# A two-layer backbone on one core: layer 1's modulation from sums on the vector engine instead of matmuls on the tensor engine

## The chip, the cores and the metric

One core of one Trainium2 chip runs the whole program. The metric is the time of one execution on the device in microseconds (us). Kernel names and line numbers (L...) are those of the kernel before, unless said otherwise; after the change the lines from 291 on are some 34 higher.

## The reference, cut to what matters

Each of the two layers modulates its inputs by six vectors that depend on a conditioning vector alone. There are two streams of tokens, 128 context tokens and 256 latent tokens, each with one conditioning vector (`c_ctx` and `c`):

```python
def adaln(cond, w, bias):
    return (jax.nn.silu(cond) @ w + bias)[:, None, :]

for l in range(DEPTH):                                    # DEPTH = 2
    mod_ctx = adaln(c_ctx[None, :], w_ada[l], b_ada[l])   # w_ada[l]: 1024 x 6144
    mod_lat = adaln(c, w_ada[l], b_ada[l])
    xp, ... = residual_block(xp, mod_ctx, p, ...)
    xs, _ = residual_block(xs, mod_lat, p, ...)

def residual_block(x, mod, p, mixer):
    sh1, sc1, g1, sh2, sc2, g2 = jnp.split(mod, 6, axis=-1)
    y, extra = mixer(rmsnorm(x, p['norm1_g']) * (1 + sc1) + sh1)
    x = x + g1 * y
    h = rmsnorm(x, p['norm2_g']) * (1 + sc2) + sh2
    x = x + g2 * (jnp.square(jax.nn.relu(h @ p['w_ff1'])) @ p['w_ff2'])
    return x, extra
```

Everything is fp32. The feed-forward is 1024 to 4096 to 1024 features for 384 tokens in all. The modulation is a product of two rows (the two streams) with a 1024 x 6144 matrix, 24 MB for each layer.

## The kernel before

Tokens lie along the free dimension: `x[k]` is tile k of 8, 128 features by T = 384 tokens. A weight matrix comes in tiles of 128x1024 (512 KB): a DMA from SyncE into `raw` (3 buffers), a rounded copy `whi` on ScalarE (L147, 3 buffers) and the remainder `wlo` on VectorE (L148, 2 buffers). `mm3` (L150 to L153) then issues three matmuls for each 128x128 block of it: `whi` by the high part of the activations, `whi` by the low part, `wlo` by the high part. A weight tile is 8 blocks, so 24 matmuls.

**The feed-forward of a layer (L1074 to L1108).** FF1 has 32 output tiles of one weight tile each. After each, VectorE reads the PSUM bank (`fb` L1089, `fa` L1090), ScalarE does the relu and the square, and the result is split into `fh` and `fl`. FF2 has 8 output tiles d, each the sum of 32 blocks, so four weight tiles (c = 0 to 3); at the end of each, `residual` (L301) adds it to `x[d]` in two VectorE instructions. FF1 and FF2 take their PSUM banks from a pool of three, tag "g".

**Layer 1's modulation** is made beside layer 0's feed-forward by the generator `ada(l + 1, [0, 1, 2])` (L272 to L290): `next(more)` runs one step of it after each FF1 tile and after each c of FF2. There are 3 rounds of 2048 columns, each 8 k by 2 halves, so 48 steps. A step is one DMA of 512 KB into `araw` (2 buffers) and 4 fp32 matmuls on TensorE, each with a 128x32 weight (`cs`, the conditioning vectors: 2 of 32 columns are not zero) by 256 columns, into a quarter of the PSUM partitions of a "g" bank. A round holds that bank for its 16 steps. The last step of a round turns the bank on VectorE (`diag`, L285) and adds the bias (`mod`, L289). The modulation of layer 0 is made elsewhere, at the start (`mraw` tiles, in `lead`) and beside layer 0's merge.

**What sets the order.** Each engine runs its instructions in the order in which a scheduler has put them. SyncE's DMA issues are in order too: a transfer whose buffer isn't free yet holds those behind it. At the start of layer 1, `modulated` (L220 to L232) makes the normalised input as a chain of VectorE instructions (L227, L230) and ScalarE ones (L229) through the 8 feature tiles, and the first matmuls of the input projection follow it tile by tile.

Of the kernel before, what the change touches and what calls it, by code (L numbers as in the profile page):

```python
# [13 lines left out]
AF = mybir.ActivationFunctionType  # L14
ALU = mybir.AluOpType
# [3 lines left out]
P = 128  # L19
DM = 1024  # L20
KT = DM // P
T = 384
SEQ = 128
DEPTH = 2
# [15 lines left out]
Q_N1, Q_N2, Q_ADA, Q_GQ, Q_GKV, Q_CW, Q_ON, Q_SINK, Q_AL, Q_DT, Q_FG = 0, 8, 16, 64, 67, 69, 105, 106, 114, 122, 130  # L40
# [4 lines left out]
def trunk(ctx: ExitStack, tc: tile.TileContext, A, O):  # L45
    nc = tc.nc
    V, S, G, PE = nc.vector, nc.scalar, nc.gpsimd, nc.tensor
    count = [0]

    def mk(pool, shape, tag, dt=F32, bufs=None):  # L50
        count[0] += 1
        return pool.tile(list(shape), dt, name=f"{tag}_{count[0]}", tag=tag, bufs=bufs)
# [28 lines left out]
    sp = sbuf("small", 2)  # L81
    dp = ctx.enter_context(tc.tile_pool(name="scratch", bufs=2, space=DRAM))
    pg = psum("pg", 3)
# [4 lines left out]
    def bank(pool=None, tag="c"):  # L88
        return mk(pc if pool is None else pool, [P, 512], tag)
# [24 lines left out]
    prm = []  # L114
# [35 lines left out]
    def mm3(ps, wh, wl, rh, rl, start, stop):  # L150
        PE.matmul(ps, lhsT=wh, rhs=rh, start=start, stop=False)  # L151
        PE.matmul(ps, lhsT=wh, rhs=rl, start=False, stop=False)  # L152
        PE.matmul(ps, lhsT=wl, rhs=rh, start=False, stop=stop)  # L153

    def mm(ps, lhsT, rhs, start=True, stop=True):
        return PE.matmul(ps, lhsT=lhsT, rhs=rhs, start=start, stop=stop)  # L156
# [103 lines left out]
    cs = mk(cp, [P, KT, 32], "cs")  # L260
# [6 lines left out]
    mods = {}  # L267
    ada_pool = [None, "araw", 2]

    def ada(l, rounds):  # L270

        for r in rounds:  # L272
            ps = bank(pg, "g")
            for k in range(KT):
                for half in range(2):
                    c0 = r * 2048 + half * 1024
                    raw = mk(ada_pool[0], [P, 1024], ada_pool[1], bufs=ada_pool[2])
                    nc.sync.dma_start(raw, A["w_ada"][l, k * P:(k + 1) * P, c0:c0 + 1024])
                    rv = raw.rearrange("p (b g i) -> p g b i", b=8, g=4)
                    for g in range(4):  # L280
                        mm(ps[32 * g:32 * g + 32, half * 256:half * 256 + 256].rearrange("p (b i) -> p b i", b=8),
                           cs[:, k, :], rv[:, g], start=k + half == 0, stop=k + half == KT)
                    if k + half == KT:
                        tr = mk(sp, [P, 512], "diag", bufs=1).rearrange("p (b i) -> p b i", b=16)
                        V.transpose(out=tr.rearrange("p b i -> p (b i)"), in_=ps)  # L285
                        m = mods[l, r] = mk(sp, [P, 16, 2], f"mod{r}")
                        bias = prm[l][:, Q_ADA + 16 * r:Q_ADA + 16 * r + 16].unsqueeze(2).to_broadcast([P, 16, 2])
                        V.tensor_tensor(out=m, in0=tr[:, :, 0:2], in1=bias, op=ALU.add)
                    yield  # L289

    def gain(m, b0, l, off, tag):
# [132 lines left out]
    for l in range(DEPTH):  # L424
# [5 lines left out]
        else:  # L430
# [6 lines left out]
            for w in weights([A["w_small"][l], A["w_in"][l, 11]]):  # L437
                wh, wl = (t.rearrange("p (k c) -> p k c", k=KT) for t in w)
                M = wh.shape[2]
                ps = mk(pg, [P, 512], "g")[:M, :T + 2]  # L440
# [4 lines left out]
            for i, ps in enumerate(pss):  # L445
                M = ps.shape[0]
                t = mk(sp, [48, T], "kab", bufs=1) if i == 0 else mk(sp, [P, T], "sqacc", bufs=1)
                b = mk(sp, [P, 2], "eb")[:M]
# [57 lines left out]
        if l == 0:  # L506
            ps, kab = kab, mk(sp, [48, T], "kab", bufs=1)
# [54 lines left out]
        for k in range(7, 0, -1):  # L562
# [4 lines left out]
        g = mk(sp, [P, 3, 8], "gdec")  # L567
        V.scalar_tensor_tensor(out=g, in0=z, scalar=-1.0, in1=nea.unsqueeze(1).to_broadcast([P, 3, 8]),
                               op0=ALU.mult, op1=ALU.mult)
# [4 lines left out]
        for d in range(2):  # L574
            for i in range(3):
# [13 lines left out]
                        op0=ALU.mult)  # L589
# [113 lines left out]
        for which, dst in enumerate((keys, queries)):  # L703
# [11 lines left out]
            r = rsqrt(v, 12, 1.0)  # L715
            r2 = mk(sp, [P, 12], f"r2{which}", bufs=1)
            if which == 0:
# [4 lines left out]
                                in1=r2.rearrange("p (n h) -> p n h", n=3).unsqueeze(2).to_broadcast([P, 3, 2, 4]), op=ALU.mult)  # L722
# [29 lines left out]
        diag = blk()  # L752
        G.memset(diag[:, :, 24:32], 0.0)
        Mg, QK, qd, ekd, ge = {}, {}, {}, {}, {}
        for n in range(3):
            Es = []
            for d in range(2):
                gr = bank()
                for h in range(4):
                    j = 8 * n + 4 * d + h  # L760
                    for i in range(3):
                        mm(gr[:, h * P:(h + 1) * P], g16[i][:, j:j + 1].to_broadcast([P, P]), tri16[:, d, :],
                           start=h + i == 0, stop=h + i == 5)
# [20 lines left out]
            for d in range(2):  # L784
                M = Mg[n, d] = g4()
                for h in range(4):
                    V.scalar_tensor_tensor(out=M[:, h, :], in0=kk[:, h * P:(h + 1) * P],
                                           scalar=beta[:, n, 4 * d + h:4 * d + h + 1], in1=Es[d][:, h, :],
                                           op0=ALU.mult, op1=ALU.mult)
# [20 lines left out]
        for j in range(31):  # L810
            r, w = 31 - j, j + 1
            tmp = flat(h4())[:, :r * w].rearrange("p (a b) -> p a b", a=r)
            V.tensor_tensor(out=tmp, in0=Cb[:, j + 1:, j:j + 1].to_broadcast([P, r, w]),  # L813
                            in1=X[:, j:j + 1, :w].to_broadcast([P, r, w]), op=ALU.mult)
# [10 lines left out]
        for n in range(3):  # L825
            for d in range(2):
# [8 lines left out]
                for dst, c in ((X0T, (Xc, XcT)[d]), (X0, (XcT, Xc)[d])):  # L835
                    V.tensor_tensor(out=dst.rearrange("p h (b c) -> p h b c", b=4),  # L836
                                    in0=c[:, u0:u0 + 4, :].unsqueeze(2).to_broadcast([P, 4, 4, 32]),
                                    in1=bdmask.rearrange("p (b c) -> p b c", b=4).unsqueeze(1).to_broadcast([P, 4, 4, 32]),
                                    op=ALU.mult)
                ps = bank()  # L840
# [237 lines left out]
        rs2 = mk(fp, [P, T], "rs2")  # L1078
        S.copy(rs2, rstd_rows(squares(x), 1.0 / DM))
        NF = 32  # L1080
        ada_pool[:] = fp, "araw", 2
        more = ada(l + 1, [0, 1, 2]) if l + 1 < DEPTH else iter(())
        ws = weights(A["w_ff1"][l, t] for t in range(NF))
        ah, al = [], []
        for t in range(NF):
# [14 lines left out]
        for d in range(KT):  # L1100
            ps = mk(pg, [P, 512], "g")
            for c in range(4):
                wh, wl = (w.rearrange("p (k c) -> p k c", k=KT) for w in next(ws))
                for k in range(KT):
                    i = c * KT + k
                    mm3(ps[:, :T], wh[:, k, :], wl[:, k, :], ah[i], al[i], i == 0, i == NF - 1)
                next(more, None)
            residual(d, ps, mod2, KT)  # L1108
        ff.close()
# [136 lines left out]
```

## Time and profile before

| | |
|---|---|
| three runs | 1579.08, 1581.01, 1582.5 us; median 1581.01 us |
| the profiled execution | 1581.47 us |
| its span in the profile | 1579.7 us, so 1.8 us lie outside of it |
| mean granted clock of TensorE in it | 0.997 |
| layer 0's feed-forward in it | 521.1 to 830.0 us |
| steps of `ada` in that stretch | 48 |

The span goes from the first instruction to the last. An engine's busy time is the sum of its instructions; matmuls overlap, so that each shows some 0.34 us while one starts every 0.175 us. A line of the timeline reads: start, duration, engine, line, operation, output<-inputs, count, and in brackets the engine's idle time before it with what ended it. Adjacent equal instructions are joined as x2, x8 and so on; one fp32 matmul shows as two records. "PE" is TensorE, "PEld" its weight load, "DVE" VectorE, "ACT" ScalarE. A row of the windows gives the stretch, its length, the busy us (and instructions) of PE, PEld, DVE, ACT and POOL, the granted clock as a share of the full one, the busy share of the DMA engines, and GB/s. A row of the groups gives line, engine, operation, names, shapes and count, then the busy us, the mean ns of one, and the idle time before them.

### The profile page before, as it was taken

The page shows a single profiled execution, that of the slowest core. Times are in us where ns is not written, and L with a number is a line of the kernel's source. Part 1 is how long each engine was busy: PE and PEld are TensorE (multiplying, and loading weights), DVE is VectorE, ACT ScalarE, POOL GpSimd, SP SyncE. Part 2 cuts the span into 40 slices and gives each one's busy share as a digit, 9 for nine tenths or more (in the row PEclk, how much of TensorE's full clock was granted, in tenths as well). Part 3 has the DMA queues.
Part 4 walks back from the last instruction along what each step waited for, and adds up shares of the span by engine and source line. Part 5 has one row for each costly group of instructions (what it writes and reads, how often), then busy time and mean ns, then how long its engine had stood idle before and what let it go on. Part 6 is the DMA issues. An engine that isn't in the chain of part 4 may idle for free.

```text
span 1579.7 us, 25197 instructions
## 1 busy us (share of the span) xinstructions
PE 1542.1 (98%) x9844; PEld 1393.1 (88%) x9844; DVE 904.4 (57%) x2016; ACT 756.1 (48%) x1498; POOL 12.9 (1%) x34
## 2 busy tenths in 40 slices
PE   5999999999999999999999999999999999999998
PEld 3898798987879888888998987989978999999997
DVE  5677995565435644443338678964755565554332
ACT  3467633446424655532325566433565456664222
POOL 0000100000000000000000001000000000000000
PEclk9999999999999999999999999999999999999999
DMA  9532131243587566666444331312423334343332
GB/s 324 157 94 94 54 94 41 68 147 98 191 274 254 166 209 209 209 216 224 155 135 123 94 99 39 118 41 65 125 69 121 120 121 134 121 125 128 128 126 80
DMA packets 73942, 212.80 MB, mean 135 GB/s; under 512 B 8032, under 2 KB 23776, under 8 KB 73696
## 3 DMA queue, kind: packets, MB, share of 16 engines
q1 hardware_dynamic: 73824, 211.21, 41.9%
q8 instruction: 77, 1.26, 0.3%
q14 instruction: 41, 0.34, 0.1%
HBM read 204.59 MB, written 4.75 MB: 133 GB/s over the span
## 4 chain that ended last, share of the span: by engine, by line
PE 88%; DVE 6%; DMA 3%; ACT 1%; issue 1%; SPq 0%; DVEq 0%; ACTq 0%
PE g L151 23%; PE g L153 22%; PE g L152 22%; PE c L156 9%; PE g L156 3%; PE f L156 3%; PE o L156 2%; PE f L409 2%; DMA araw<-in_w_ada_dram 2%; DVE wlo L148 1%; DVE h L813 1%; DVE blk L815 1%; DMA mraw<-in_w_ada_dram 1%; PE c L151 1%; PE c L153 1%
## 5 line engine op out<-in xcount | busy, mean ns | idle before, releaser
L147 ACT CAST whi<-raw 128x1024 fp32r<-128x1024 f32 x268 | 280.6, 1047 | 503.5 <-PE g L152 449.2
L151 PE MATMUL g<-hh,whi 128*128 128x384 f32 (+1 forms) x1440 | 495.6, 346 | 2.2 <-ACT bq L679 1.3
L153 PE MATMUL g<-hh,wlo 128*128 128x384 f32 (+1 forms) x1440 | 493.5, 344 | 2.8 <-DVE wlo L148 2.8
L152 PE MATMUL g<-hl,whi 128*128 128x384 f32 (+1 forms) x1440 | 490.8, 342 | 0.0
L148 DVE TENSOR_TENSOR wlo<-raw,whi 128x1024 fp32r<-128x1024 f32 x268 | 326.2, 1217 | 230.0 <-PE g L153 183.1
L151 PEld LDWEIGHTS g<-hh,whi 128*128 128x128 f32 x1440 | 270.9, 188 | 25.3 <-issue 17.0
L153 PEld LDWEIGHTS g<-hh,wlo 128*128 128x128 f32 x1440 | 271.0, 188 | 12.8 <-DVE wlo L148 6.1
L152 PEld LDWEIGHTS g<-hl,whi 128*128 128x128 f32 x1440 | 271.1, 188 | 4.7 <-issue 2.7
L151 PE MATMUL g<-fh,whi 128*128 128x384 f32 x512 | 174.1, 340 | 0.0
L153 PE MATMUL g<-fh,wlo 128*128 128x384 f32 x512 | 172.2, 336 | 0.0
L152 PE MATMUL g<-fl,whi 128*128 128x384 f32 x512 | 172.2, 336 | 0.0
L151 PEld LDWEIGHTS g<-fh,whi 128*128 128x128 f32 x512 | 96.4, 188 | 7.0 <-issue 7.0
L152 PEld LDWEIGHTS g<-fl,whi 128*128 128x128 f32 x512 | 96.5, 188 | 0.0
L153 PEld LDWEIGHTS g<-fh,wlo 128*128 128x128 f32 x512 | 96.4, 188 | 0.0
L156 PE MATMUL c<-g,g 128*128 128x128 f32 (+1 forms) x608 | 77.6, 274 | 3.7 <-DVE g L836 3.1
L156 PEld LDWEIGHTS c<-g,g 128*128 128x128 f32 (+1 forms) x608 | 69.9, 183 | 11.5 <-ACT g L844 4.0
L301 DVE SCALAR_TENSOR_TENSOR x<-g,mod,x 128x128 f32<-128x128 f32 x64 | 23.8, 413 | 80.0 <-PE g L153 80.0
L148 DVE TENSOR_TENSOR fl<-fa,fh 128x384 fp32r<-128x384 f32 x64 | 35.7, 559 | 58.7 <-ACT fh L147 58.7
L151 PE MATMUL g<-brh,whi 128*128 128x384 f32 x192 | 66.4, 346 | 0.4 <-ACT whi L147 0.4
L152 PE MATMUL g<-brl,whi 128*128 128x384 f32 x192 | 65.8, 343 | 0.0
L153 PE MATMUL g<-brh,wlo 128*128 128x384 f32 x192 | 65.7, 342 | 0.0
L390 ACT ACTIVATE at_p<-at_p,at_nm 128x384 f32<-128x384 f32 (+1 forms) x96 | 51.8, 541 | 24.1 <-DVE at_nm L387 23.4
(306 smaller groups left out, 1848.8 us busy)
## 6 DMA issues: line engine op xcount, KB each, us to landing
raw<-in_w_ff_dram SPq DMA_DIRECT2D x128, 512.0 KB, 3.8
raw<-in_w_in_dram SPq DMA_DIRECT2D x102, 512.0 KB, 3.6
araw<-in_w_ada_dram SPq DMA_DIRECT2D x72, 512.0 KB, 4.0
raw<-in_w_branch_dram SPq DMA_DIRECT2D x24, 512.0 KB, 3.6
raw<-in_w_out_dram SPq DMA_DIRECT2D x16, 512.0 KB, 3.6
mraw<-in_w_ada_dram SPq DMA_DIRECT2D x8, 512.0 KB, 9.3
mraw<-in_w_ada_dram SPq DMA_DIRECT2D x16, 256.0 KB, 7.1
raw<-in_w_ada_dram SPq DMA_DIRECT2D x8, 512.0 KB, 4.1
```

The lines of the kernel that those rows point to most:

```text
L147: S.copy(hi, src)
L148: V.tensor_tensor(out=lo, in0=src, in1=hi.bitcast(F32), op=ALU.subtract)
L151: PE.matmul(ps, lhsT=wh, rhs=rh, start=start, stop=False)
L152: PE.matmul(ps, lhsT=wh, rhs=rl, start=False, stop=False)
L153: PE.matmul(ps, lhsT=wl, rhs=rh, start=False, stop=stop)
L156: return PE.matmul(ps, lhsT=lhsT, rhs=rhs, start=start, stop=stop)
L301: V.scalar_tensor_tensor(out=x[k][:, c], in0=ps[:, c], scalar=m[:, b0 + k, s:s + 1], in1=x[k][:, c], op0=ALU.mult, op1=ALU.add)
L390: S.activation(sm[:, :nk], sm[:, :nk], AF.Exp, bias=nm[:, u:u + 1], scale=-1.0, accum_out=den[:, u:u + 1])
L409: PE.transpose(pt[:, j * P:(j + 1) * P], ps_[half, n][:, c * P:(c + 1) * P], ident)
L813: V.tensor_tensor(out=tmp, in0=Cb[:, j + 1:, j:j + 1].to_broadcast([P, r, w]), in1=X[:, j:j + 1, :w].to_broadcast([P, r, w]), op=ALU.mult)
L815: V.tensor_tensor(out=X[:, j + 1:, :w], in0=X[:, j + 1:, :w], in1=tmp, op=ALU.subtract)
```

## The change

`ada_sums` takes the place of `ada` beside layer 0's feed-forward. The sum over the 8 feature tiles k is now made with the products on VectorE: for each stream, `acc = araw * cs + acc`, where `cs` is one number for each partition. Only the sum over the 128 partitions is left to TensorE.

- The 6144 columns are taken as 3 rounds of 4 quarters of 512 columns, each through 8 k: 96 steps. A step is one DMA of 256 KB into `araw` (128x512, 3 buffers) and two instructions (one for each stream) of 128x512: for k = 0 on ScalarE (`activation` with the scale `cs`), for the other seven on VectorE (`scalar_tensor_tensor`). That makes 24 instructions on ScalarE and 168 on VectorE. Both streams of a quarter share one buffer `aacc` (128x2x512, 1 buffer).
- After k = 7 of a quarter, 8 fp32 matmuls with a 128x32 weight (`pick`: one column of ones in a place for the stream) by 128 columns sum `aacc` over the partitions. There are 12 such groups instead of 48 groups of 4 by 256 columns.
- `next(more)` is called once for each FF1 tile as before, and twice instead of once for each c of FF2: 32 + 64 = 96 steps. One quarter of columns ends with every eighth FF1 tile, and one with each d of FF2.
- The end of a round (transpose and bias) is the same code, moved into `modulation`. Three memsets make `pick`.

The diff, without the removed lines that came back in `modulation`:

```diff
+    def modulation(l, r, ps):
+        tr = mk(sp, [P, 512], "diag", bufs=1).rearrange("p (b i) -> p b i", b=16)
+        V.transpose(out=tr.rearrange("p b i -> p (b i)"), in_=ps)
...
+    def ada_sums(l, rounds, pool):
+        pick = mk(pool, [P, 2, 32], "pick")
+        V.memset(pick, 0.0)
+        for s in range(2):
+            V.memset(pick[:, s, s:s + 1], 1.0)
+        for r in rounds:
+            ps = bank(pg, "g")
+            for q in range(4):
+                acc = mk(pool, [P, 2, 512], "aacc", bufs=1)
+                c0 = r * 2048 + q * 512
+                for k in range(KT):
+                    raw = mk(pool, [P, 512], "araw", bufs=3)
+                    nc.sync.dma_start(raw, A["w_ada"][l, k * P:(k + 1) * P, c0:c0 + 512])
+                    for s in range(2):
+                        if k == 0:
+                            S.activation(acc[:, s, :], raw, AF.Copy, scale=cs[:, k, s:s + 1])
+                        else:
+                            V.scalar_tensor_tensor(out=acc[:, s, :], in0=raw, scalar=cs[:, k, s:s + 1], in1=acc[:, s, :],
+                                                   op0=ALU.mult, op1=ALU.add)
+                    if k == KT - 1:
+                        for s in range(2):
+                            av = acc[:, s, :].rearrange("p (b g i) -> p g b i", b=4, g=4)
+                            for g in range(4):
+                                mm(ps[32 * g:32 * g + 32, q * 128:q * 128 + 128].rearrange("p (b i) -> p b i", b=4),
+                                   pick[:, s, :], av[:, g], start=q + s == 0, stop=q + s == 4)
+                        if q == 3:
+                            modulation(l, r, ps)
+                    yield
...
-        ada_pool[:] = fp, "araw", 2
-        more = ada(l + 1, [0, 1, 2]) if l + 1 < DEPTH else iter(())
+        more = ada_sums(l + 1, [0, 1, 2], fp) if l + 1 < DEPTH else iter(())
...
                     mm3(ps[:, :T], wh[:, k, :], wl[:, k, :], ah[i], al[i], i == 0, i == NF - 1)
                 next(more, None)
+                next(more, None)
             residual(d, ps, mod2, KT)
```

**Where the instructions go.** TensorE before, inside FF2, between two c of the second d (`fh_`, `fl_` are the activations, `whi_`, `wlo_` the two parts of a weight tile; "x4" joins the four matmuls of a step):

```order
L151 MATMUL g_7096<-fh_6161,whi_7135 128x384
L152 MATMUL g_7096<-fl_6162,whi_7135 128x384
L153 MATMUL g_7096<-fh_6161,wlo_7136 128x384
L156 MATMUL g_6979<-araw_7163,cs_93 32x256 x4
L151 MATMUL g_7096<-fh_6213,whi_7171 128x384
L152 MATMUL g_7096<-fl_6214,whi_7171 128x384
```

TensorE of the change, inside FF2, where the first d (`g_6919`) ends and the second (`g_7084`) begins:

```order
L151 MATMUL g_6919<-fh_6899,whi_7038 128x384
L152 MATMUL g_6919<-fl_6900,whi_7038 128x384
L153 MATMUL g_6919<-fh_6899,wlo_7039 128x384
L156 MATMUL g_6950<-aacc_6951,pick_5444 32x128 x8
L151 MATMUL g_7084<-fh_5440,whi_7087 128x384
```

A group of four stood after every weight tile. Now a group of eight shorter ones stands after every eighth FF1 tile and after every d, and nothing between.

VectorE before, inside FF2, from the end of one d on (`sqacc` and `hl` belong to the input of layer 1):

```order
L301 SCALAR_TENSOR_TENSOR x_991_4993<-g_7096,mod_973_4952,x_991_4993 128x128
L301 SCALAR_TENSOR_TENSOR x_991_4993<-g_7096,mod_973_4952,x_991_4993 128x256
L148 TENSOR_TENSOR wlo_7283<-raw_7280,whi_7282 128x1024
L215 TENSOR_TENSOR sqacc_8034<-sqacc_8034,tmp_8036 128x384
L243 SCALAR_TENSOR_TENSOR hl_8104<-x_991_4993,gp_1499_8093,hh_8103 128x128
L243 SCALAR_TENSOR_TENSOR hl_8104<-x_991_4993,gp_1499_8093,hh_8103 128x256
L148 TENSOR_TENSOR hl_8112<-mod_1211_6173,hh_8111 128x2
L148 TENSOR_TENSOR wlo_7319<-raw_7316,whi_7318 128x1024
```

VectorE of the change at the same place ("x2" joins the two streams):

```order
L148 TENSOR_TENSOR wlo_7291<-raw_7288,whi_7290 128x1024
L313 SCALAR_TENSOR_TENSOR aacc_7279<-araw_7284,cs_93,aacc_7279 128x512 x2
L313 SCALAR_TENSOR_TENSOR aacc_7279<-araw_7318,cs_93,aacc_7279 128x512 x2
L215 TENSOR_TENSOR sqacc_8242<-sqacc_8242,tmp_8244 128x384
L148 TENSOR_TENSOR wlo_7329<-raw_7326,whi_7328 128x1024
L313 SCALAR_TENSOR_TENSOR aacc_7279<-araw_7322,cs_93,aacc_7279 128x512 x2
L313 SCALAR_TENSOR_TENSOR aacc_7279<-araw_7356,cs_93,aacc_7279 128x512 x2
L313 SCALAR_TENSOR_TENSOR aacc_7279<-araw_7360,cs_93,aacc_7279 128x512 x2
L148 TENSOR_TENSOR wlo_7367<-raw_7364,whi_7366 128x1024
L313 SCALAR_TENSOR_TENSOR aacc_7279<-araw_7394,cs_93,aacc_7279 128x512 x2
L313 SCALAR_TENSOR_TENSOR aacc_7279<-araw_7398,cs_93,aacc_7279 128x512 x2
L148 TENSOR_TENSOR wlo_7416<-raw_7413,whi_7415 128x1024
```

The seven pairs of products now stand between the four `wlo` of a d; three of them stand in one run ahead of the third `wlo`.

VectorE before, at the start of layer 1, in the middle of the chain of `modulated`:

```order
L227 SCALAR_TENSOR_TENSOR tmp_8248<-x_993_4995,gp_1499_8093,c_8083 128x128
L227 SCALAR_TENSOR_TENSOR tmp_8248<-x_993_4995,gp_1499_8093,c_8083 128x256
L449 COPY eb_8301<-g_8196 128x2
L148 TENSOR_TENSOR wlo_8454<-raw_8451,whi_8453 128x1024
L230 SCALAR_TENSOR_TENSOR hl_8241<-tmp_8239,mod_1211_6173,hh_8240 128x128
```

VectorE of the change there, at the chain's end:

```order
L230 SCALAR_TENSOR_TENSOR hl_8494<-tmp_8492,mod_1360_6917,hh_8493 128x128
L230 SCALAR_TENSOR_TENSOR hl_8494<-tmp_8492,mod_1360_6917,hh_8493 128x256
L485 TENSOR_TENSOR kab_8501<-kab_8501,c_8291 48x384
L483 COPY eb_8509<-g_8404 128x2
L148 TENSOR_TENSOR wlo_8662<-raw_8659,whi_8661 128x1024
L148 TENSOR_TENSOR wlo_8704<-raw_8701,whi_8703 128x1024
```

The `wlo` of a weight tile of the input projection, which stood inside the chain, stands behind the whole of it.

## Rows read from the trace of the kernel before

**Rows 1.** The page, part 1 (busy time) and part 4 (chain that ended last).

```profile
PE 1542.1 (98%) x9844; PEld 1393.1 (88%) x9844; DVE 904.4 (57%) x2016; ACT 756.1 (48%) x1498; POOL 12.9 (1%) x34
...
PE 88%; DVE 6%; DMA 3%; ACT 1%; issue 1%; SPq 0%; DVEq 0%; ACTq 0%
```

**Rows 2.** Windows, feed-forward with steps: busy us, then PEclk, DMA share, GB/s.

```profile
537.00:765.00 228.00, 228.00 (x1462) 198.02 (x1461) 97.95 (x164) 107.07 (x188) 0.00 (x0) 1.00 0.65 210
```

**Rows 3.** Timeline: FF1 of layer 0, end of a tile and a step.

```profile
558.68 0.16 DVE L1089 COPY fb<-g 128x2 f32<-128x2 f32 x1 [1.75 <-PE g L153]
...
563.58 0.64 PE L156 MATMUL g<-araw,cs 128*32 128x256 f32 x8
563.69 0.16 DVE L1089 COPY fb<-g 128x2 f32<-128x2 f32 x1 [1.74 <-PE g L153]
...
564.15 0.44 PE L151 MATMUL g<-hh,whi 128*128 128x386 f32 x1
```

**Rows 4.** Timeline of VectorE: FF1 of layer 1, which has no steps.

```profile
1333.32 0.16 DVE L1089 COPY fb<-g 128x2 f32<-128x2 f32 x1 [0.97 <-PE g L153]
...
1337.55 0.16 DVE L1089 COPY fb<-g 128x2 f32<-128x2 f32 x1 [0.97 <-PE g L153]
```

**Rows 5.** Timeline of VectorE: FF2 of layer 0, two rows with steps, then without.

```profile
693.77 1.23 DVE L148 TENSOR_TENSOR wlo<-raw,whi 128x1024 fp32r<-128x1024 f32 x1 [3.76 <-PE g L153]
698.70 1.23 DVE L148 TENSOR_TENSOR wlo<-raw,whi 128x1024 fp32r<-128x1024 f32 x1 [3.71 <-PE g L153]
...
780.19 0.74 DVE L301 SCALAR_TENSOR_TENSOR x<-g,mod,x 128x128 f32<-128x128 f32 x2 [2.88 <-PE g L153]
780.85 1.21 DVE L148 TENSOR_TENSOR wlo<-raw,whi 128x1024 fp32r<-128x1024 f32 x1
781.99 0.55 DVE L215 TENSOR_TENSOR sqacc<-sqacc,tmp 128x384 f32<-128x384 f32 x1
...
796.83 0.74 DVE L301 SCALAR_TENSOR_TENSOR x<-g,mod,x 128x128 f32<-128x128 f32 x2 [2.88 <-PE g L153]
```

**Rows 6.** Timeline of TensorE: layer 0's start, groups of 128 columns, 32-wide weights.

```profile
38.36 0.86 PE L156 MATMUL c<-mraw,cs 128*32 128x128 f32 x24
39.16 0.38 PE L151 MATMUL g<-hh,lhi 128*48 128x384 f32 x1
...
43.65 0.43 PE L156 MATMUL c<-mraw,cs 128*32 128x128 f32 x8
44.00 0.44 PE L152 MATMUL g<-hl,lhi 128*128 128x384 f32 x1
```

**Rows 7.** Groups of VectorE by form: scalar_tensor_tensor with a scalar per partition.

```profile
L243 DVE SCALAR_TENSOR_TENSOR hl<-x,gp,hh 128x256 fp32r<-128x256 f32 x24 | 11.5, 478 | 0.0
...
L663 DVE SCALAR_TENSOR_TENSOR brz<-brz,prm,g 128x384 f32<-128x384 f32 x8 | 4.9, 612 | 0.1
```

**Rows 8.** Timeline of VectorE: layer 1's convolution, two updates of one tile in place.

```profile
951.14 0.34 DVE L598 SCALAR_TENSOR_TENSOR g<-g,cw,g 128x127 f32<-128x127 f32 x1
951.52 0.35 DVE L600 SCALAR_TENSOR_TENSOR g<-g,cw,g 128x127 f32<-128x127 f32 x1
```

**Rows 9.** DMA of 684 to 765: KB each, median us from issue to landing.

```profile
raw<-in_w_ff_dram SPq DMA_DIRECT2D x16, 512.0 KB, 4.8
araw<-in_w_ada_dram SPq DMA_DIRECT2D x15, 512.0 KB, 4.0
```

**Rows 10.** DMA of 0 to 45, the start of layer 0: the same columns.

```profile
mraw<-in_w_ada_dram SPq DMA_DIRECT2D x16, 256.0 KB, 7.1
```

**Rows 11.** Timeline of VectorE: start of layer 1, the chain's first link and its `wlo`.

```profile
837.07 0.99 DVE L227 SCALAR_TENSOR_TENSOR tmp<-x,gp,c 128x128 f32<-128x128 f32 x3
...
841.06 1.22 DVE L148 TENSOR_TENSOR wlo<-raw,whi 128x1024 fp32r<-128x1024 f32 x1
...
849.89 2.36 DVE L148 TENSOR_TENSOR wlo<-raw,whi 128x1024 fp32r<-128x1024 f32 x2
```

**Rows 12.** Groups of VectorE by form: the transpose at a round's end.

```profile
L285 DVE STREAM_TRANSPOSE diag<-g 128x512 f32<-128x512 f32 x5 | 3.6, 711 | 0.0
```

More of the change, by code (lines that the diff above doesn't have):

```diff
@@ L268, in trunk @@
     ada_pool = [None, "araw", 2]
+    def modulation(l, r, ps):
+        tr = mk(sp, [P, 512], "diag", bufs=1).rearrange("p (b i) -> p b i", b=16)
+        V.transpose(out=tr.rearrange("p b i -> p (b i)"), in_=ps)
+        m = mods[l, r] = mk(sp, [P, 16, 2], f"mod{r}")
+        bias = prm[l][:, Q_ADA + 16 * r:Q_ADA + 16 * r + 16].unsqueeze(2).to_broadcast([P, 16, 2])
+        V.tensor_tensor(out=m, in0=tr[:, :, 0:2], in1=bias, op=ALU.add)
     def ada(l, rounds):
@@ L283, in ada @@
                     if k + half == KT:
[L284 to L288, printed above, removed]
+                        modulation(l, r, ps)
[26 more added lines that the diff above has]
+                        if q == 3:
+                            modulation(l, r, ps)
                     yield
```

## The prediction

> **What bounds the kernel now.** I read the page first. TensorE is busy for 98% of the span, VectorE for 57%, ScalarE for 48%, and 88% of the chain that ended last lies on TensorE [rows 1]. So what counts is what leaves TensorE, and whether the engine that takes the work stays behind it. Then the windows of layer 0's feed-forward: with steps of `ada`, TensorE is busy for all of 228 us at the full granted clock (1.00, the 2.4 GHz level), VectorE for 98 and ScalarE for 107, and the DMA engines are at a share of 0.65 with 210 GB/s [rows 2]. TensorE is the bound of this stretch, and every instruction that leaves it there should be saved whole. Then the timeline, for what one step costs: an FF1 tile with a step takes 563.69 − 558.68 = 5.01 us from `fb` to `fb` [rows 3], one without 1337.55 − 1333.32 = 4.23 us [rows 4]. In FF2 a weight tile with a step takes 698.70 − 693.77 = 4.93 us, and a d of four tiles without one 796.83 − 780.19 = 16.64 us, or 4.16 for a tile [rows 5]. Either way a step costs 0.77 us.
>
> **The change, part by part.** The sum is made against the profiled execution, 1581.5 us; the median of the runs is 1581.0, so I take the same difference from the median.
>
> *Removed from TensorE:* 48 steps by 0.77 us = **−37.0 us**. TensorE has no wait there that could swallow it.
>
> *Added to TensorE:* 12 groups with `pick`. No row shows this group, but its nearest kin are the `mraw` groups with the same 32-wide weight and 128 columns: four matmuls last 44.00 − 43.65 = 0.35 us until the next starts, twelve 39.16 − 38.36 = 0.80, so four more cost 0.22 [rows 6], and eight take 0.57. An old step held TensorE for 564.15 − 563.58 = 0.57 us and cost 0.77 [rows 3], so 0.20 us of change-over come on top: 0.77 for a group, 12 × 0.77 = **+9.2 us**. From below it is 12 × 0.57 = 6.8, from above two separate groups of four with a change-over each, 12 × 1.10 = 13.2. I take 9.2, since the eight stand in one piece, as the twelve do.
>
> *Added to VectorE:* 168 `scalar_tensor_tensor` of 128x512. The same operation with a scalar for each partition takes 478 ns for 256 columns and 612 for 384 [rows 7], 134 ns for each further 128, so some 0.746 us for 512. But an instruction that depends on nothing running starts before its forerunner's end: the pair of `residual` lasts 0.74 us and the next instruction starts after 0.66, and a `wlo` of 1.21 is followed after 1.14 [rows 5]. That is 0.08 us less each, so 0.66 us from start to start. The order alternates the streams, so no product directly follows the one it needs.
>
> The tight place is FF2, where each d has seven pairs: 14 × 0.66 = 9.3 us. With four `wlo` at 1.14 (4.6), the residual (0.66), `sqacc` (0.46, from 781.99 to the next) and `hl` (0.7) [rows 5], VectorE needs 15.7 us for a d. TensorE needs 16.64 + 0.77 = 17.4. VectorE stays under it, at 90%, where it was under half. FF1 is easy: the seven pairs are spread over eight tiles of some 4.3 us. So these products cost **0**, as long as the weight tiles cover them: the `wlo` of a d come out some 2 us ahead of their use. If that cover goes, TensorE waits for `wlo`, at first at the third tile of a d, ahead of which three pairs stand in a run.
>
> ScalarE gets 24 instructions, two for each of twelve quarters; in FF2 they stand behind a `whi`, at the start of a d, when ScalarE has least to do. They cost 0, hidden by ScalarE's idle time (it works for 107 of 228 us [rows 2]).
>
> *Transfers:* the bytes are the same, in 96 pieces of 256 KB. In FF2 a d now brings 2 MB of weights and 2 MB of `araw` in 17.4 us instead of 19.7, some 240 GB/s where there were 210, at a share that rises from 0.65 to about 0.74. That alone costs 0. But a product now holds a buffer until VectorE has it, and there are three: a refill is issued when a buffer comes free, and SyncE issues in order, so what waits there also holds the weight tiles behind it. I laid out one d by hand with a landing of 4.0 us, as the `araw` of 512 KB show now [rows 9]: the fourth product (k = 3) starts about 6.8 us after the start of the d, the seventh (k = 6) about 12.3, the last is done at 14.9, and every `wlo` is ready 1.5 to 2 us early. With 4.8 us, as the weight tiles show [rows 9], it still just fits. I take 0, and the bounds are 0 and +16 (a landing of 6 us; below).
>
> *The start of layer 1.* Here the order gets worse. Before, one `wlo` of the input projection stood inside the chain of `modulated` (841.06, in a chain from 837.07 to the last `wlo` at 849.89 [rows 11]), so TensorE had two weight tiles to work on as the links came out. Now this `wlo` stands behind the whole chain, with the next one: TensorE follows the chain with one tile, and another tile of 24 matmuls at 0.175 us, 4.2 us, goes behind it. The chain itself gets shorter by the `wlo` it no longer holds (842.19 − 841.06 = 1.1 us), and starts later by the transpose of the last round, 0.7 us [rows 12], which stands ahead of it, for the last group of `pick` ends only with the last d. 4.2 − 1.1 + 0.7 = **+3.8 us**. It could be 0, if TensorE loses the same time now by waiting for the links, or +6, if both later `wlo` are waited for.
>
> **The sum:** −37.0 + 9.2 + 3.8 = −24.0 us, so **1557 us**. With the bounds of the groups and of layer 1's start alone it lies between 1551 and 1563.
>
> **The rivals.**
>
> *A, VectorE becomes the bound of FF2.* At 90% of TensorE's time with fixed order there is little room. An instruction that needs its forerunner's result starts only behind its end: two updates of one tile stand 951.52 − 951.14 = 0.38 us apart, where one lasts 0.34 [rows 8]. If the products were held like that, 0.75 + 0.04 = 0.79 us each, a d would be 14 × 0.13 = 1.8 us longer on VectorE, 17.5 us, above TensorE's 17.4; with a wait of about a microsecond for a landing in each d, the loss is 1 us by 8 d in FF2, and **1565**. The streams alternate, which speaks against it. The Trainium skill (VectorE: DVE Perf Modes, "The DRAIN you can't avoid") says that after every VectorE instruction the next waits until the pipe is empty; by that rule products would follow at their full duration and a d would be 16.8 us, still just under TensorE, and the starts before the end in this trace speak against it for instructions that don't hang together.
>
> *B, the refills of `araw` come late: slower.* With three buffers VectorE waits twice in a d for a landing, ahead of k = 3 and of k = 6, and each microsecond of landing beyond the 5 that fit goes into both: up to 2 us in each of 8 d, 16 us in all. At 6 us that is 1573, at 6.5 the whole saving is gone, and at the 7.1 us which pieces of 256 KB took in the start of layer 0 [rows 10] it is 2.1 × 16 = 34 us, **1591**. There all queues were full of transfers; the 4.0 and 4.8 us at 0.65 of load [rows 9] speak against it, the higher share in FF2 and the order on SyncE for a part of it.
>
> *C, the start of layer 1 loses nothing* and the groups cost their lower bound: 1581.0 − 37.0 + 6.8 = **1551**.
>
> *D, the change takes less from TensorE than it says.* The group of 8 × 128 columns has as many columns as an old step, and if each of its two halves is a change-over of its own the sum is 4 us worse, **1561**; it can't undo the saving, for there are 12 instead of 48.
>
> **How the numbers follow.** 0.2%, 3.2 us, is about what can be told from no change. The forecast, with C and D inside its own range of 1551 to 1563, gets 0.66; A (1563 to 1570) 0.16; B 0.18, of which a third is a mild form up to 1577 that is still faster, 0.04 lie within 3.2 us, and 0.08 are slower. So faster 0.88, same 0.04, slower 0.08. The range goes from 1551 to 1572 and leaves out the upper part of B and a little below: 2 in 10.
>
> **What would show it.** *Right:* in the windows, layer 0's feed-forward is some 28 us shorter, with TensorE busy throughout and VectorE near 90% in FF2; `fb` to `fb` is 4.23 us but for every eighth tile, at 5.0; a d of FF2 takes 17.4 us from residual to residual; twelve groups with `pick` show 0.6 us each; the three tiles at the start of layer 1 end some 4 us later after the last residual than before. *Wrong:* A, if products stand back to back at 0.79 us and TensorE waits for `wlo` on VectorE; B, if the products of L313 wait for the DMA of `araw` and its landing is over 5 us; and the sum itself, if the time from the last residual of layer 0 to the end of layer 1 changes by more than the 6 us allowed.

## The result, and the profile after

The changed kernel takes 1563.4 us (median of four runs, 1563.1 to 1564.5), the kernel before, measured beside it, 1581.8: a ratio of 0.9888, with an interval from 0.9871 to 0.9905. So it is faster by 18 us, and not by the forecast 24. The profiled execution has a span of 1562.7 us.

The page of the changed kernel, parts 1, 4, 5 and 6, to be read beside [rows 1, 9]; L313 is the product in `ada_sums`:

```profile
PE 1521.6 (97%) x9652; PEld 1396.2 (89%) x9652; DVE 1013.9 (65%) x2187; ACT 771.8 (49%) x1522; POOL 12.9 (1%) x34
...
PE 86%; DVE 8%; DMA 4%; ACT 1%; issue 1%; SPq 0%; DVEq 0%; ACTq 0%
...
L313 DVE SCALAR_TENSOR_TENSOR aacc<-araw,cs,aacc 128x512 f32<-128x512 f32 x168 | 116.5, 747 | 11.0 <-DMA araw<-in_w_ada_dram 6.9
...
araw<-in_w_ada_dram SPq DMA_DIRECT2D x96, 256.0 KB, 3.4
```

TensorE is still the bound. VectorE has 110 us more; a product takes 747 ns, where 746 were worked out.

**The feed-forward came out as forecast.** Windows of the changed kernel: eight tiles of FF1, one d of FF2, and the last two d, beside [rows 2]:

```profile
566.00:601.00 35.00, 35.00 (x212) 34.54 (x211) 27.60 (x48) 23.77 (x43) 0.00 (x0) 1.00 0.59 183
700.00:718.00 18.00, 18.00 (x130) 17.35 (x129) 15.83 (x24) 7.21 (x11) 0.00 (x0) 1.00 0.77 249
770.00:805.00 35.00, 35.00 (x237) 34.02 (x228) 31.17 (x50) 12.90 (x21) 0.31 (x1) 1.00 0.73 230
```

TensorE is busy all the time, VectorE for 79% in FF1 and 88 to 89% in FF2. In the timeline of VectorE, FF1 (L1122 is `fb`), the tile of 4.24 us shows as in [rows 4], and once in eight tiles a longer one:

```profile
591.72 0.16 DVE L1122 COPY fb<-g 128x2 f32<-128x2 f32 x1 [0.97 <-PE g L153]
595.96 0.16 DVE L1122 COPY fb<-g 128x2 f32<-128x2 f32 x1 [0.97 <-PE g L153]
601.42 0.15 DVE L1122 COPY fb<-g 128x2 f32<-128x2 f32 x1
605.20 0.16 DVE L1122 COPY fb<-g 128x2 f32<-128x2 f32 x1 [0.23 <-PE g L153]
```

The 5.46 us hold a group of `pick` and a product ahead of `fb`; the next interval, 3.78, gives back what the product held up. The timeline of TensorE at the end of a d shows the group itself, beside [rows 3, 6]: 0.57 us from its start to the next matmul's, as worked out.

```profile
787.12 0.64 PE L156 MATMUL g<-aacc,pick 128*32 128x128 f32 x16
787.69 0.45 PE L151 MATMUL g<-fh,whi 128*128 128x384 f32 x1
```

FF2 from residual to residual (L335), and one d of it on VectorE, beside [rows 5]:

```profile
682.66 0.74 DVE L335 SCALAR_TENSOR_TENSOR x<-g,mod,x 128x128 f32<-128x128 f32 x2 [0.69 <-PE g L153]
...
700.09 0.74 DVE L335 SCALAR_TENSOR_TENSOR x<-g,mod,x 128x128 f32<-128x128 f32 x2 [0.50 <-PE g L153]
700.75 1.22 DVE L148 TENSOR_TENSOR wlo<-raw,whi 128x1024 fp32r<-128x1024 f32 x1
701.88 2.73 DVE L313 SCALAR_TENSOR_TENSOR aacc<-araw,cs,aacc 128x512 f32<-128x512 f32 x4
704.53 0.55 DVE L215 TENSOR_TENSOR sqacc<-sqacc,tmp 128x384 f32<-128x384 f32 x1
705.03 1.23 DVE L148 TENSOR_TENSOR wlo<-raw,whi 128x1024 fp32r<-128x1024 f32 x1
707.68 4.07 DVE L313 SCALAR_TENSOR_TENSOR aacc<-araw,cs,aacc 128x512 f32<-128x512 f32 x6 [1.42 <-DMA araw<-in_w_ada_dram]
711.66 1.22 DVE L148 TENSOR_TENSOR wlo<-raw,whi 128x1024 fp32r<-128x1024 f32 x1
713.54 2.74 DVE L313 SCALAR_TENSOR_TENSOR aacc<-araw,cs,aacc 128x512 f32<-128x512 f32 x4 [0.66 <-DMA araw<-in_w_ada_dram]
...
804.65 0.74 DVE L335 SCALAR_TENSOR_TENSOR x<-g,mod,x 128x128 f32<-128x128 f32 x2 [2.29 <-PE g L153]
```

(804.65 − 682.66) / 7 = 17.43 us for a d; 17.4 was the forecast. Six products take 4.07 us, the last of them 0.75, so (4.07 − 0.75) / 5 = 0.66 us from start to start. This is one of the fullest d: VectorE waits for `araw` twice, at the two places of the layout by hand (ahead of k = 3 and of k = 6), and still TensorE waits for nothing in FF2.

**The loss lies behind it.** From the last residual of layer 0 to the span's end it is 1579.7 − 830.11 = 749.6 us before and 1562.7 − 804.65 = 758.0 after: 8.4 us longer, where 3.8 were forecast. VectorE there, beside [rows 11]:

```profile
813.30 1.00 DVE L227 SCALAR_TENSOR_TENSOR tmp<-x,gp,c 128x128 f32<-128x128 f32 x3 [0.79 <-PE c L156]
...
824.59 2.34 DVE L148 TENSOR_TENSOR wlo<-raw,whi 128x1024 fp32r<-128x1024 f32 x2
```

The chain starts 8.65 us after the last residual (6.96 before), and both `wlo` follow its end, 19.94 us after the last residual. Before, one `wlo` stood inside the chain and the next two behind it, from 19.78 us on [rows 11]. Windows of the changed kernel from the last residual on, and the timeline of TensorE inside the fourth of them:

```profile
804.60:812.60 8.00, 8.00 (x65) 6.30 (x64) 6.41 (x23) 3.46 (x6) 0.00 (x0) 1.00 0.49 155
812.60:818.00 5.40, 5.04 (x32) 4.37 (x31) 4.54 (x14) 3.89 (x9) 0.00 (x0) 1.00 0.63 191
818.00:823.00 5.00, 3.24 (x12) 1.91 (x12) 5.00 (x17) 3.27 (x8) 0.00 (x0) 1.00 0.01 3
823.00:833.50 10.50, 9.05 (x28) 7.73 (x28) 8.11 (x26) 4.38 (x12) 0.00 (x0) 0.51 0.34 108
833.50:860.00 26.50, 26.50 (x162) 24.92 (x162) 16.64 (x48) 11.65 (x23) 0.00 (x0) 1.00 0.32 103
```

```profile
828.68 0.52 PE L151 MATMUL g<-hh,whi 128*128 128x384 f32 x1
829.00 0.52 PE L152 MATMUL g<-hl,whi 128*128 128x384 f32 x1
```

The first number behind POOL is the granted clock. TensorE works 3.24 of 5.00 us in the chain; then the clock is at 0.51, the 1.2 GHz level, for 10.5 us, and a matmul starts every 0.32 us instead of every 0.175. The transfers all but stop in the chain (a share of 0.01), but they are not what is waited for: ScalarE stands idle for 1.59 us ahead of the next `whi` (825.22) and VectorE for 3.47 us ahead of the next `wlo` (835.40), both until TensorE has done with a buffer. Windows of the kernel before at the same distance from its last residual: the clock stays at 1.00.

```profile
830.00:838.00 8.00, 8.00 (x56) 6.18 (x55) 6.50 (x24) 4.02 (x8) 0.00 (x0) 1.00 0.36 107
838.00:843.00 5.00, 4.69 (x27) 4.22 (x25) 5.00 (x15) 3.56 (x9) 0.00 (x0) 1.00 0.33 105
843.00:848.00 5.00, 4.73 (x28) 4.56 (x27) 5.00 (x16) 3.47 (x10) 0.00 (x0) 1.00 0.72 213
848.00:858.00 10.00, 9.29 (x55) 8.75 (x54) 8.39 (x23) 6.89 (x16) 0.00 (x0) 1.00 0.38 120
```

### The profile page after: what moved, and what is told of

The parts are those of the page before. It is cut to its first block, busy times and chain, and to the rows that moved or that the text cites. A ratio compares the mean times of both kernels' runs of the same rounds, so it can differ in the third digit from the quotient of the medians.

```text
span 1562.7 us, 25131 instructions
## 1 busy us (share of the span) xinstructions
PE 1521.6 (97%) x9652; PEld 1396.2 (89%) x9652; DVE 1013.9 (65%) x2187; ACT 771.8 (49%) x1522; POOL 12.9 (1%) x34
## 4 chain that ended last, share of the span: by engine, by line
PE 86%; DVE 8%; DMA 4%; ACT 1%; issue 1%; SPq 0%; DVEq 0%; ACTq 0%
PE g L151 22%; PE g L153 22%; PE g L152 22%; PE c L156 9%; PE f L156 3%; DMA araw<-in_w_ada_dram 2%; PE o L156 2%; PE f L443 2%; DVE wlo L148 2%; PE g L156 1%; DVE h L847 1%; DVE blk L849 1%; DMA mraw<-in_w_ada_dram 1%; PE c L151 1%; PE c L153 1%
## 5 line engine op out<-in xcount | busy, mean ns | idle before, releaser
L153 PE MATMUL g<-hh,wlo 128*128 128x384 f32 (+1 forms) x1440 | 495.2, 345 | 2.8 <-DVE wlo L148 2.7
L151 PEld LDWEIGHTS g<-hh,whi 128*128 128x128 f32 x1440 | 272.2, 189 | 14.9 <-issue 6.3
L313 DVE SCALAR_TENSOR_TENSOR aacc<-araw,cs,aacc 128x512 f32<-128x512 f32 x168 | 116.5, 747 | 11.0 <-DMA araw<-in_w_ada_dram 6.9
```

The lines of the kernel that those rows point to most:

```text
L313: V.scalar_tensor_tensor(out=acc[:, s, :], in0=raw, scalar=cs[:, k, s:s + 1], in1=acc[:, s, :], op0=ALU.mult, op1=ALU.add)
```

## The experiments

Theory 1 after the result: the feed-forward gained its 28 us; what is missing was lost at the start of layer 1, about half by the order there and half by the clock that falls when TensorE waits. Its rivals put the loss on the products and transfers, on the order alone without the clock, or on the last group of `pick` and the last transpose. Each run has two readings: its ratio to the kernel before, and in its profile the time from the last residual of layer 0 to the eleventh `wlo` after it (52.5 us before, 60.9 after) and to the span's end. The first stretch holds the whole start of layer 1. The ratios come from several executions of each kernel, the two stretches from one profiled execution each.

| kernel | ratio to before (interval) | to the 11th `wlo` | to the end |
|---|---|---|---|
| before | 1 | 52.5 | 749.6 |
| the change | 0.9888 (0.9871 to 0.9905) | 60.9 | 758.0 |
| last quarter one d earlier | 0.9826 (0.9809 to 0.9843) | 52.4 | 750.3 |
| filler in the chain | 0.9864 (0.9848 to 0.9881) | 56.5 | 753.8 |
| no products | 0.9879 (0.9864 to 0.9894) | 60.9 | 758.0 |
| two buffers | 1.0011 (0.9999 to 1.0023) | 60.3 | 758.3 |
| `wlo` ahead of the chain's middle | 0.9854 (0.9840 to 0.9867) | 54.6 | 753.4 |
| extra products | 1.0118 (1.0104 to 1.0132) | 64.5 | 763.4 |
| last quarter two d earlier | 0.9827 (0.9813 to 0.9842) | 52.4 | 749.0 |
| one d earlier and `wlo` ahead | 0.9837 (0.9823 to 0.9851) | 53.6 | 750.4 |
| before, with a late `wlo` | 1.0026 (1.0013 to 1.0038) | 59.5 | 755.8 |

**The last quarter one d earlier.**

```diff
             al.append(lo)
             next(more, None)
+            if t % 4 == 3:
+                next(more, None)
```

> The changed kernel with one more step after every fourth tile of FF1, so that the last quarter of columns ends with the seventh d instead of the eighth. The wlo of the input projection then stands inside the chain of modulated again, as before the change, and the last transpose long before it. Theory 1 (the feed-forward gained its 28 us, and what was lost lies at the start of layer 1: about 4 us by the order and about 4.5 by the clock, which fell to 0.50 after TensorE had waited in the chain): from the last residual of layer 0 to the third wlo behind the chain the time is as before the change, the granted clock stays at 1.00 there, and the whole is 7 to 9 us faster than the changed kernel, 1555 us. Rival (the products or the transfers of the sums, which still fill FF2, hold up what follows): no more than 3 us are gained, 1560 to 1563.

Measured: 1555.0 us, ratio 0.9826; against 0.9888 that is 0.0062 × 1582 = 9.8 us faster than the change, a little over the 7 to 9 expected. Windows from its last residual (807.0) on:

```profile
815.00:820.00 5.00, 4.69 (x26) 4.08 (x24) 5.00 (x15) 3.56 (x9) 0.00 (x0) 1.00 0.37 105
820.00:825.00 5.00, 4.73 (x28) 4.71 (x28) 5.00 (x17) 3.48 (x9) 0.00 (x0) 1.00 0.73 210
825.00:835.00 10.00, 9.29 (x54) 8.75 (x53) 8.37 (x24) 6.74 (x16) 0.00 (x0) 1.00 0.37 120
```

They are those of the kernel before, almost to the digit, with the clock at 1.00. The products fill FF2 as in the change, but for the last d. So the loss hangs on the start of layer 1, and the order there is got back without touching it.

**Filler in the chain.** Three matmuls behind each link, into a bank that nothing reads.

```diff
+            if spare is not None:
+                for i in range(3):
+                    PE.matmul(spare[:, :T], lhsT=hi[:, :P], rhs=hi[:, :T], start=i == 0, stop=i == 2)
             his.append(hi)
```

> The changed kernel with three more matmuls behind each link of layer 1's chain, into a bank that nobody reads; the order of VectorE stays that of the change. They fill TensorE's waits in the chain. Theory 1: the granted clock stays at 1.00 from the chain on, the matmuls behind it start every 0.175 us instead of every 0.32, and the whole is 4 to 5 us faster than the changed kernel, 1559 us, though TensorE has 24 matmuls more. Rival 1 (the order alone costs the 8.4 us, and the low clock only stands beside waits): the same time as the changed kernel within 1 us, or up to 2 us more.

Measured: 1561.6 us, ratio 0.9864, 3.8 us faster than the change, though the two intervals just overlap. The order is as bad as there, and TensorE has 24 matmuls more, but:

```profile
810.40:816.00 5.60, 5.60 (x37) 5.48 (x37) 4.82 (x15) 4.17 (x9) 0.00 (x0) 1.00 0.61 187
816.00:821.00 5.00, 4.81 (x28) 4.31 (x27) 5.00 (x16) 3.15 (x9) 0.00 (x0) 1.00 0.00 0
821.00:831.00 10.00, 9.84 (x56) 9.22 (x55) 9.80 (x32) 6.02 (x15) 0.00 (x0) 1.00 0.40 115
```

The clock stays at 1.00, and the start of layer 1 is 4.4 us shorter (56.5 against 60.9). That is the price of the low clock by itself. It was not an accident of one profile: the mean granted clock over the whole program lies between 0.991 and 0.994 in the four executions of the change, and between 0.995 and 0.997 in the four with the filler. The other 4.0 us against the kernel before are still there: the chain, and what stands behind it.

**No products.** k = 1 to 6 are left out with their transfers, so the modulation of layer 1 lacks these terms.

```diff
                 for k in range(KT):
+                    if 0 < k < KT - 1:
+                        yield
+                        continue
                     raw = mk(pool, [P, 512], "araw", bufs=3)
```

> The changed kernel without the products of k = 1 to 6 and without their transfers (18 of 24 MB are not read, the modulation of layer 1 is wrong by these terms); the groups with pick, the transposes and the order at the start of layer 1 stay. Theory 1 (VectorE and the transfers have room enough in the feed-forward): a d of FF2 still takes 17.4 us, and the whole is within 2 us of the changed kernel, 1561 to 1564. Rival 2 (the products load VectorE so that TensorE or the chain waits for it): at least 4 us faster.

Measured: 1563.8 us, ratio 0.9879, 1.4 us faster than the change, with intervals that overlap. A d takes (803.35 − 681.36) / 7 = 17.43 us, and the start of layer 1 is as long as in the change. What VectorE does in the feed-forward costs 309.9 − 309.0 = 0.9 us from the first residual of the stage of w_out to the last of layer 0, and by the ratios 1.4 us, which can't be told from nothing.

**Two buffers for `araw`.** `bufs=3` becomes `bufs=2`.

> The changed kernel with two buffers for araw instead of three. It prices the rival of late refills. Theory 1: a refill is then on the path: a landing of 3.4 us plus issue and two products (1.3) for two steps make 2.5 to 2.8 us a step, where FF2 has 2.18 for one; a d takes 20 to 22 us instead of 17.4, some 20 to 35 us more, 1585 to 1600; FF1, with one step in 4.3 us, does not change. Rival (buffers are not what keeps the products going, the transfers overlap anyway): within 3 us of the changed kernel.

Measured: 1586.1 us, ratio 1.0011: the whole gain is gone. Against the change that is 0.0123 × 1582 = 19.5 us, just under the 20 to 35 expected. One d of it on VectorE:

```profile
765.81 0.74 DVE L335 SCALAR_TENSOR_TENSOR x<-g,mod,x 128x128 f32<-128x128 f32 x2
...
778.25 2.74 DVE L313 SCALAR_TENSOR_TENSOR aacc<-araw,cs,aacc 128x512 f32<-128x512 f32 x4 [0.56 <-DMA araw<-in_w_ada_dram]
780.90 1.22 DVE L148 TENSOR_TENSOR wlo<-raw,whi 128x1024 fp32r<-128x1024 f32 x1
783.23 2.74 DVE L313 SCALAR_TENSOR_TENSOR aacc<-araw,cs,aacc 128x512 f32<-128x512 f32 x4 [1.11 <-DMA araw<-in_w_ada_dram]
785.88 0.73 DVE L335 SCALAR_TENSOR_TENSOR x<-g,mod,x 128x128 f32<-128x128 f32 x2
```

20.1 us for this d instead of 17.4; the mean of seven is (826.60 − 684.57) / 7 = 20.3. The products wait for landings. TensorE then waits for the products, at the place where its order has `pick`. All its waits in these seven d are one row (who waited for whom, us in total, times, longest):

```profile
PE g L156 <- DVE aacc L313: 11.8, 12, 2.3
```

It never waits for `wlo` there. The granted clock is 0.95 in these seven d, where it was 1.00 in the change, so a part of the 20 us that they lose is again the clock's. The late landings are rival B of the prediction, at two buffers; with three TensorE waits for none of them.

**`wlo` ahead of the chain's middle.** The sums stay as in the change; only the order at the start of layer 1 is mended.

```diff
+            wpre = weights(A["w_in"][l, t] for t in range(11))
+            ahead = [next(wpre), next(wpre)]
             hh, hl = modulated(rb, gp1, mod0, 0)
...
-            ws = win(0, 11)
+            ws = win(0, 11) if l == 0 else (w for g in (ahead, wpre) for w in g)
```

> The changed kernel, its sums untouched (the last quarter still ends with the last d, the last transpose stands ahead of the chain), but the first two weight tiles that follow layer 1's chain are split ahead of the chain in the code, so that both wlo stand before or inside it. It undoes the order alone. Theory 1 (the wlo behind the chain leaves TensorE one tile to work on; that costs about 4 us by itself and 4 more because TensorE waits and its clock falls): the granted clock stays at 1.00, the time from the last residual of layer 0 to the end falls from 758.0 to 750 to 752 us, and the whole is 6 to 8 us faster than the changed kernel. Rival (the transpose and the last group of pick, which stand ahead of the chain, cost it): that time stays within 2 us of 758.

Measured: 1559.2 us, ratio 0.9854, 5.4 us faster than the change, and 753.4 us to the end: a little less gained than expected in both. The clock keeps its level though the last group of `pick` and the transpose still stand ahead of the chain:

```profile
811.60:817.00 5.40, 5.13 (x34) 4.62 (x34) 4.45 (x11) 3.17 (x7) 0.00 (x0) 1.00 0.30 97
817.00:822.00 5.00, 4.47 (x22) 3.32 (x22) 5.00 (x17) 3.18 (x8) 0.00 (x0) 1.00 0.69 210
822.00:832.00 10.00, 9.10 (x51) 7.99 (x50) 9.59 (x30) 7.39 (x18) 0.00 (x0) 1.00 0.34 101
```

The start is 54.6 us long, 6.3 less than in the change and 2.1 more than before.

**Both remedies, and two d earlier.** The first adds the extra step after every fourth FF1 tile to the kernel just shown; the second puts an extra step after every second tile.

> The run with one d earlier, and the two weight tiles split ahead of layer 1's chain in the code. Theory 1: either remedy restores the order, so both together give what the run with one d earlier gives, within 2 us (0.9826 of the kernel before). Rival (each takes away a different loss): 3 us or more faster than the run with one d earlier.

> The changed kernel with one more step after every second tile of FF1, so that the last quarter ends with the sixth d. As the run with one d earlier, with more of the products in FF1. Theory 1: the start of layer 1 is as before the change, and the total is that of the run with one d earlier within 2 us, since TensorE has the same work and is waited for nowhere. Rival (FF1 has less room than FF2, its fb and fa stand behind products): 2 to 6 us slower than the run with one d earlier.

Measured: 0.9837 and 0.9827, both the same as one d earlier within their intervals, so the remedies do not add up, and FF1 takes more products without a loss that the ratios show. Both remedies together leave 53.6 us to the eleventh `wlo`, 1.0 less than the `wlo` alone: this is what the last group and the last transpose cost where they stand ahead of the chain. The other 1.1 us against the kernel before remain in both kernels with this remedy; no run takes them apart.

**Extra products.** One more for each k from 1, with a scalar of zero.

```diff
+                    if k:
+                        V.scalar_tensor_tensor(out=acc[:, 0, :], in0=raw, scalar=cs[:, k, 2:3], in1=acc[:, 0, :],
+                                               op0=ALU.mult, op1=ALU.add)
                     if k == KT - 1:
```

> The changed kernel with one product more for each k from 1 to 7 (a product with zero that leaves the sum as it is): 7 for each quarter, 84 in all. It asks where VectorE becomes the bound. A d has 15.7 us of work on VectorE by the sum of the prediction and 17.4 on TensorE. Theory 1: with 7 by 0.66 to 0.75 us more VectorE needs 20.3 to 21 us and sets the pace, so a d takes 20 to 21.5 us instead of 17.4 and the whole is 20 to 35 us slower than the changed kernel; FF1, with room for them, keeps its pace. Rival (VectorE has far more room than the sum says): a d stays under 18.5 us.

Measured: 1601.3 us, ratio 1.0118, 36 us slower than the change, a little over the upper bound. Two ends of a d:

```profile
796.83 0.34 DVE L338 SCALAR_TENSOR_TENSOR x<-g,mod,x 128x128 f32<-128x128 f32 x1
...
817.08 0.35 DVE L338 SCALAR_TENSOR_TENSOR x<-g,mod,x 128x128 f32<-128x128 f32 x1
```

This d takes 20.2 us, the mean of seven (from 686.72 to 837.12) is 21.5, with single ones between 18.3 and 25.0. VectorE sets the pace now: it is busy for 142.4 of the 150.4 us of the seven. (21.5 − 17.4) × 8 = 33 us are from there, and 5 more from a start of layer 1 that is longer still (763.4 us to the end). TensorE's waits in the seven d:

```profile
PE g L156 <- DVE aacc L316: 12.0, 4, 5.6
```

Besides, it waits 8.0 us for `wlo`, in four places, and its clock is 0.95 in the mean. L316 is the added product.

**The kernel before, with a late `wlo`.** No sums on VectorE at all; the edit names the whole projection of that weight tile, but in the trace its `wlo` goes behind the chain's last link, while its `whi` keeps its place (5.3 us after the last residual in both kernels).

```diff
-            ps = project(ws)
+            if l == 0:
+                ps = project(ws)
+            else:
+                with tc.issue_after(end[0].ins):
+                    ps = project(ws)
```

> The kernel before the change, its matmuls for the modulation untouched, but the wlo of the weight tile that stood inside layer 1's chain is held behind the chain's last link, as the order of the change has it. Theory 1 (this place in the order is what costs, by TensorE's waits and by the clock that falls after them; the sums have no part in it): the granted clock falls to 0.50 for about 10 us behind the chain, the time from the last residual of layer 0 to the end grows from 749.6 to 754 to 757 us, and the whole is 5 to 7 us slower than the kernel before, 1587 to 1590. Rival (the last transpose and the last group of pick, which this kernel does not have there, are needed for the loss): within 2 us of the kernel before, clock at 1.00.

Measured: 1588.0 us, ratio 1.0026, 4.1 us slower than the kernel before, with an interval from 2 to 6 us: the sign and the place as expected, the size under it. Its profiled execution (last residual at 833.26), the longest of six and the one with the lowest mean clock (0.992, for 0.994 to 0.996 in the others), is 6.2 us longer behind the last residual, and 7.0 of the change's 8.4 us show at the eleventh `wlo`:

```profile
841.00:846.00 5.00, 4.66 (x25) 4.08 (x24) 4.13 (x14) 3.56 (x9) 0.00 (x0) 1.00 0.71 208
846.00:851.00 5.00, 3.69 (x14) 2.21 (x14) 5.00 (x16) 3.66 (x10) 0.00 (x0) 0.99 0.00 1
851.00:861.00 10.00, 8.55 (x26) 7.79 (x27) 8.58 (x28) 4.92 (x13) 0.00 (x0) 0.50 0.37 116
861.00:888.00 27.00, 27.00 (x163) 24.88 (x162) 16.25 (x44) 11.43 (x22) 0.00 (x0) 1.00 0.35 100
```

The same picture in the old kernel: TensorE works 3.69 of 5.00 us, then the clock is at 0.50 for 10 us. The sums have no part in it but that they moved the order. Whether the clock fell as far in the shorter executions is not shown.

## Why the prediction was right, and where it was wrong

- **Removed from TensorE, −37.0, and the groups, +9.2:** right. From the first residual of the stage of w_out to the last of layer 0 the time falls from 830.11 − 492.01 = 338.1 to 804.65 − 494.72 = 309.9 us, so by 28.2, where the two terms give 27.8. A group costs 17.43 − 16.64 = 0.79 us, for 0.77.
- **The products, 0:** right. 0.66 us from start to start and 747 ns each are as worked out from [rows 7] and the pair of `residual`. Leaving most of them out is worth 1.4 us, within the intervals. The rule of the Trainium skill as the prediction quotes it (VectorE: DVE Perf Modes, "The DRAIN you can't avoid") would give 0.75 from start to start; the trace doesn't agree for products that alternate between two sums. The same section of the Trainium skill goes on to say that a next operation that is not held starts earlier, and with that the 0.66 us agree. That rival A would decide with more work is shown: with 4.6 us more for a d VectorE sets the pace. What I had wrong there is the path: I let TensorE wait for `wlo`, and it waits first for the last sums, ahead of `pick` (11.8 us with two buffers and none for `wlo`; 12.0 against 8.0 with the extra products).
- **The products' place:** I had the first quarter spread over eight FF1 tiles; in the trace its products begin in the stage of w_out (the first at 503.11). They stand ahead of residuals there, and from the first residual to the last that stage takes 29.9 us, for 29.4 before and 29.4 again in the run without most of the products: 0.6 us that the prediction didn't have.
- **The refills, 0:** right, with less room than said. `araw` lands after 3.4 us, not 4.0; in the full d shown above the fourth product starts 707.68 − 700.09 = 7.6 us after the residual, for 6.8 by hand, and the last ends at 16.2, for 14.9. TensorE did not wait. With two buffers rival B eats the gain.
- **The start of layer 1, +3.8: the step that failed, by its size.** It measured 8.4 us. The place and the order were right: with the clock held up by the filler, the start is 4.0 us longer than before, though not by the sum I gave: the chain starts 1.7 us later, not 0.7, and the `wlo` behind it come 0.2 us later than before, where 0.7 − 1.1 would have them 0.4 us earlier. That 3.8 comes so near to 4.0 is in part luck. What I left out is that TensorE, waiting link by link, also loses its clock, which costs another 4.4 us. Holding the order of the change against its repair, the late `wlo` costs 60.9 − 54.6 = 6.3 us with the clock in it, the last group and the transpose 1.0. So the upper bound of that term, 6, was too low too, since it allowed for waits alone.
- **The sum:** the two parts give −28.2 + 8.4 = −19.8 us. The spans of the two profiles differ by 17.0 and the medians by 18.4. The rest is within what the part ahead of w_out's stage differs from one execution to the next: the first residual of that stage stands at 492.0 us in the profile before and at 494.7 in the one after, and between 490.7 and 496.0 in all the profiles here, with 495.2 in the old kernel with the late `wlo`.
- **The rivals:** none of them came. C's opposite did: the start of layer 1 lost more than its bounds.

## What to carry to other kernels

When work leaves the engine that bounds a stage, price the seam behind the stage as closely as the stage: what ended last there moves, and the scheduler may put a weight tile's `wlo` behind a chain that it stood in. Look, too, at where the engine that was relieved still waits for the moved work: here, with two buffers, TensorE waited at `pick` for the last sums and never for a `wlo`. Let the moved work end a little before the stage does (here one d: 1555 us instead of 1563) and the old order comes back. Where the bounding engine is about to wait in small pieces, ask the granted clock in the windows behind the wait, and price the stretch at the lower level as well.

## What the hardware showed that I had not expected

TensorE never waited for more than 0.6 us at a time in the chain, and yet the clock fell to half at its end, for some 10 us in which it had work most of the time (9.05 of 10.5 us busy): in the change after 5 us with 3.24 busy, in the old kernel with the late `wlo` after 5 us with 3.69 busy. In the runs that mended the order the waits there were shorter (4.47 and 4.73 of 5.00 us busy) and it stayed at 1.00, and 24 useless matmuls in the gaps kept it there in the changed kernel, which was then 3.8 us faster by the ratios.

Elsewhere the clock differs between executions that do the same. Windows some 148 us behind the last residual, of the run with one d earlier and, as a row of its own, of the kernel before:

```profile
955.00:970.00 15.00, 12.99 (x67) 12.11 (x66) 13.41 (x35) 9.54 (x20) 1.98 (x5) 0.89 0.24 70
```

```profile
978.00:993.00 15.00, 12.97 (x77) 12.03 (x77) 14.62 (x39) 10.22 (x21) 2.20 (x5) 1.00 0.26 75
```

TensorE shows as busy in both, 12.99 and 12.97 of 15 us, but it gets through 67 matmuls in the one and 77 in the other, for the clock is 0.89 in the one and 1.00 in the other. It cost the one profile 1.4 us, and the run with the `wlo` ahead of the chain's middle as much at the same place (clock 0.89); that is most of what its time to the end has over the kernel before beyond the 2.1 us at the start of layer 1. Why these executions fell and others not stays open.
